# Conformer convolution module: one written order of TensorE, VectorE and ScalarE between its two projections, the last gated block multiplied token tile by token tile, and the low part of the bias row made on GpSimd

## The chip, the cores and the metric

The kernel runs on one core of one Trainium2 chip. The metric is the device time of one execution in microseconds; a median of several executions is given. Engines are named as in the profile: PE (TensorE, matrix multiplications and transposes), ACT (ScalarE), DVE (VectorE), POOL (GpSimd) and SP (SyncE, which here only issues DMAs).

## The reference, cut to what matters

The program is a two-layer trunk over 256 latent tokens (and 256 context tokens in layer one) of width 1024. Layer one mixes tokens with a state-space scan, layer two with a Conformer convolution module; a SwiGLU feed-forward network (FFN) follows each. The change lies in layer two's convolution module:

```
def conformer_conv_module(h, rows, w_pw1, b_pw1, dw_w, dw_b, ln_g, ln_b, w_pw2, b_pw2):
    u = h @ w_pw1 + b_pw1
    u = u[..., :CONF_DIM] * jax.nn.sigmoid(u[..., CONF_DIM:])
    v = axial_dwconv(u, rows, dw_w, dw_b)
    v = jax.nn.silu(layernorm(v, ln_g, ln_b))
    return v @ w_pw2 + b_pw2
...
h_lat = h_lat + g1 * y_lat
```

The 256 tokens are a grid of 4 rows of 64. The depthwise convolution has 31 taps. The first 512 channels are convolved along the rows of the grid ("horizontal": 31 taps within a row of 64). The other 512 are convolved along its columns ("vertical"): a column has 4 tokens, so at most 7 taps matter. The LayerNorm runs over the 1024 channels of one token, so that it needs all eight channel blocks of 128 of a token before it can begin.

## The kernel before, in words

**Numbers.** Every 32-bit projection is done with three TensorE products: a weight tile is split into a high part `wh` (a cast on ACT, L269) and a low part `wl` (a subtraction on DVE, L282), the activation likewise into `xmh` and `xml` (L298, L299), and L293 to L295 add wh·xmh, wl·xmh and wh·xml. A weight tile of 128x1024 thus costs a DMA issued by SP (L267), one ACT instruction and one DVE instruction. The raw tiles have a ring of buffers, so that a late tile's DMA waits until an earlier tile's subtraction has read its buffer.

**First projection.** `tok_proj` (L725) multiplies one of four blocks j of 256 value and 256 gate channels: four weight tiles q, and for each the 6 matmuls of token tile 0 and the 6 of token tile 1, 48 matmuls of 512 columns in all. The tokens stand on the partitions of the result `acc`. ACT copies each token tile of it to `ug` (L1119). After the second weight tile of the next block, PE turns the block before (transposes to `ps`, L250), ACT makes the sigmoid of the gate half (`sig`, L1106) and DVE multiplies (L1108). Blocks j = 0 and 1 give the channel blocks 0 to 3 (into `upad`, padded for the row convolution), j = 2 and 3 the blocks 4 to 7 (into `uver`).

**Depthwise convolution.** A vertical block is one ACT instruction (L1086) and six DVE instructions (L1089) that each add one tap to `cv`. Of the horizontal blocks, block 0 is done wholly on DVE (31 taps, L1139, in two alternating sums `cv` and `odd` that L1141 adds). Blocks 1 and 2 are done wholly on PE and block 3 to 20 of its 31 taps: `upad` goes out to DRAM and comes back as four shifted copies `u4` (DMAs, L1148 and L1150), and `horizontal` (L1153) multiplies these with small diagonal matrices (L1159), 32 matmuls for each block and token tile (20 for block 3). Two rows of the grid are one token tile, 128 columns. ACT moves the result of blocks 1 and 2 to `cv` (L1163), DVE adds that of block 3 (L1165). In the trace a matmul of 32-bit data counts as two, so that 32 of them read "x64".

**LayerNorm and second projection.** For each token tile, `stats` turns two channel blocks at a time to have tokens on partitions (L250, into `acc`) and takes BN_STATS of each 256 channels (DVE, L194). `root` joins them (L198, `var` on L450, `rstd` on GpSimd, L443). `rows` normalizes (L204), `channels` turns it back (L250) and applies gain, bias and SiLU on ACT (L216), `split` makes xmh and xml. Then `project` (L505) multiplies with eight tiles of w_pw2 into four result quarters (2 token tiles by 2 halves of the channels), after two matmuls for each quarter that put in the bias from the two rows `bh` and `bl` (L543). The last four weight tiles come quarter by quarter, "ends". Each quarter is multiplied with the gate row `grow` (L562) and added to the stream `h` (L566); the first FFN norm follows. `grow` comes by a GpSimd DMA (L429) that is written to be issued after the newest `rstd`.

**What sets the order.** Around the first projection only PE's order is written out; the other engines are placed by a scheduler by priority. From the LayerNorm on, a written order of tokens holds for PE, DVE, ACT and POOL together: `LNO`, where `s02` is stats of token tile 0 for the channel blocks 4 and 5, `r` is root, `m` rows, `c` channels, `x` split, `h30` the horizontal block 3 for token tile 0, `W0` the load of w_pw2's tile 0 with its cast, `w0` its subtraction, and `t` a load of ACT's table for SiLU. Then `ORDER` takes over: `R00` is L562/L566 of token tile 0 and channel half 0, `T` the transposes of the FFN norm. `CO` puts one horizontal, block 1 of token tile 0, ahead of `LNO`. The weights w_pw2 4 to 7 are placed by the scheduler, whose freedom is limited by `LF`.

Of the kernel before, what the change touches and what calls it, by code (L numbers as in the profile page):

```python
# [47 lines left out]
LF = (4, 8, "x01"),  # L48
# [4 lines left out]
CO = (1, 0, 2),  # L53
LNO = "W0 w0 W1 w1 s02 s12 h20 h30 t00 s03 s00 s01 r00 W2 W3 s13 h11 m00 c00 m01 w2 c01 h21 x00 w3 s10 x01 m02 c02 m03 c03 x02 x03 h31 s11 r10 m10 c10 m11 c11 x10 m12 x11 m13 c12 x12 c13 x13"
# [121 lines left out]
class LayerNorm:  # L176
# [31 lines left out]
    def channels(self, p, g, b):  # L208
# [14 lines left out]
class Trunk:  # L223
# [501 lines left out]
    def tok_proj(self, src, xh, xl, by_tile=False, between=lambda: None):  # L725
# [345 lines left out]
    def conformer(self, es, xh, xl, h, then):  # L1071
# [12 lines left out]
        def vertical(blk, u):  # L1084
            o = rows(cv[:, blk])
            self.vmark = nc.scalar.activation(out=o, in_=u, func=AF.Identity, scale=w(15, blk), bias=col(PC_DWB + blk)).ins  # L1086
            for d in (-3, -2, -1, 1, 2, 3):
                a, b = max(0, -d), 4 - max(0, d)
                j = nc.vector.scalar_tensor_tensor(out=o[:, a:b], in0=u[:, a + d:b + d], scalar=w(15 + d, blk),  # L1089
                                                   in1=o[:, a:b], op0=ALU.mult, op1=ALU.add)  # L1090
            return j.ins
# [4 lines left out]
        def gated(j, ug):  # L1096

            for b in range(2):
                blk = 2 * j + b
                pt = self.bank()  # L1100
                for s in range(2):
                    for tt in range(2):
                        self.transpose(pt[:, s * 256 + tt * P:s * 256 + tt * P + P],
                                       ug[:, tt, s * 256 + b * P:s * 256 + b * P + P])
                sig = cp.tile([P, 256], F32, name="sig", bufs=2)
                nc.scalar.activation(out=sig, in_=pt[:, 256:512], func=AF.Sigmoid, bias=col(PC_BPW1 + 8 + blk))  # L1106
                u = rows(up[:, blk, 0:376]) if blk < 4 else cp.tile([P, 4, 64], F32, name="uver", bufs=4)
                nc.vector.scalar_tensor_tensor(out=u[:, :, 15:79] if blk < 4 else u, in0=rows(pt[:, 0:256]),  # L1108
                                               scalar=col(PC_BPW1 + blk), in1=rows(sig), op0=ALU.add, op1=ALU.mult)
# [199 lines left out]
```

## Time and profile before

| | us |
|---|---|
| median of 3 runs | 891.5 |
| lowest, highest | 891.26, 891.66 |
| the profiled execution | 889.17 |
| its span in the profile | 887.4 |
| first matmul of block j = 3 | 623.7 |
| last matmul of block j = 3 | 637.7 |
| first matmul of the second projection | 659.1 |
| first transposes of the FFN norm (T00) | 686.96 |

The span of the profiled execution is 1.77 us shorter than its time; the times in the views are counted from the span's start. The program takes the region from 623 to 687 us once. The mean granted clock of TensorE over the whole span is 0.989 of the full speed. PE is busy for 853.3 us of the span (96%), DVE for 665.2, ACT for 506.6 and POOL for 50.6. Rows of a timeline read: start, duration, engine, line, operation, result and sources, and in brackets how long the engine had been idle ahead of it and what ended that.

### The profile page before, as it was taken

What the parts mean: (1) busy time and instruction counts of PE and PEld (TensorE: products, weight loads), DVE (VectorE), ACT (ScalarE), POOL (GpSimd) and SP (SyncE); (2) the same over time, 40 slices, a digit from 0 to 9 for tenths busy, and PEclk for the clock granted to TensorE, in tenths of its full rate; (3) what the DMA queues carried; (4) which work ended last, traced back from release to release, by engine and by line L of the source; (5) the groups of instructions that cost most, each with busy time, mean ns of one, the idle gap of its engine ahead of it and who ended that gap; (6) DMA issues with size and microseconds to landing.
All of it is one profiled execution on the core that took longest, in us unless ns stands there. A gap on an engine that the chain in (4) does not pass through costs nothing.

```text
span 887.4 us, 12716 instructions
## 1 busy us (share of the span) xinstructions
PE 853.3 (96%) x4634; PEld 650.0 (73%) x4634; DVE 665.2 (75%) x1095; ACT 506.6 (57%) x851; POOL 50.6 (6%) x78
## 2 busy tenths in 40 slices
PE   8999999999999999899999999999989999999996
PEld 4576776767677777677888877878767788888885
DVE  3378689897788989879888899677966895555434
ACT  4276988786777987465434444557353754444321
POOL 1001010101011011110000000010001000000000
PEclk9999999999999999989999999999989999999999
DMA  9757856758454445548999888828635497555521
GB/s 342 312 168 253 258 186 197 249 159 262 137 184 167 162 159 179 164 147 308 384 331 368 313 324 325 277 76 296 162 132 202 144 332 255 174 187 188 188 76 47
DMA packets 55873, 194.59 MB, mean 219 GB/s; under 512 B 6666, under 2 KB 9170, under 8 KB 54787
## 3 DMA queue, kind: packets, MB, share of 16 engines
q1 hardware_dynamic: 54338, 190.00, 62.5%
q0 software_dynamic: 896, 2.28, 0.8%
q10 hardware_dynamic: 576, 1.51, 0.6%
q8 instruction: 36, 0.59, 0.3%
q14 instruction: 27, 0.21, 0.1%
HBM read 191.94 MB, written 1.82 MB: 218 GB/s over the span
## 4 chain that ended last, share of the span: by engine, by line
PE 61%; DVE 17%; ACT 6%; DMA 5%; issue 3%; POOL 2%; POOLq 0%; SPq 0%; DVEq 0%; ACTq 0%
PE acc L295 17%; PE acc L294 17%; PE acc L293 17%; DVE wl L282 4%; DVE bx L722 3%; PE ps L250 2%; ACT wh L269 2%; PE ps L970 1%; PE ps L1000 1%; DMA wraw<-in_w_z_dram 1%; DMA wraw<-in_w_pw_dram 1%; PE ps L1159 1%; POOL yw L1014 1%; DMA emat<-edram 1%; PE ps L1008 1%
## 5 line engine op out<-in xcount | busy, mean ns | idle before, releaser
L282 DVE TENSOR_TENSOR wl<-wraw,wh 128x1024 fp32r<-128x1024 f32 (+2 forms) x229 | 269.5, 1183 | 96.8 <-ACT wh L269 96.1
L269 ACT CAST wh<-wraw 128x1024 fp32r<-128x1024 f32 (+2 forms) x229 | 231.1, 1017 | 164.3 <-PE acc L295 70.2
L293 PE MATMUL acc<-wh,xmh 128*128 128x512 f32 x544 | 218.6, 402 | 1.7 <-ACT bx L715 1.4
L295 PE MATMUL acc<-wh,xml 128*128 128x512 f32 x544 | 214.5, 395 | 0.9 <-DVE xml L299 0.8
L294 PE MATMUL acc<-wl,xmh 128*128 128x512 f32 x544 | 214.4, 394 | 0.5 <-DVE wl L282 0.4
L293 PEld LDWEIGHTS acc<-wh,xmh 128*128 128x128 f32 x544 | 102.2, 188 | 29.8 <-issue 4.8
L295 PEld LDWEIGHTS acc<-wh,xml 128*128 128x128 f32 x544 | 102.2, 188 | 26.4 <-DVE xml L299 3.4
L294 PEld LDWEIGHTS acc<-wl,xmh 128*128 128x128 f32 x544 | 102.4, 188 | 22.4 <-DVE wl L282 1.8
L293 PE MATMUL acc<-xmh,wh 128*128 128x512 f32 (+1 forms) x192 | 77.4, 403 | 0.0
L295 PE MATMUL acc<-xmh,wl 128*128 128x512 f32 (+1 forms) x192 | 75.8, 395 | 0.3 <-DVE wl L282 0.3
L294 PE MATMUL acc<-xml,wh 128*128 128x512 f32 (+1 forms) x192 | 75.9, 395 | 0.0
L722 DVE SCALAR_TENSOR_TENSOR bx<-bxraw,pc,bx 128x508 f32<-128x508 f32 (+1 forms) x96 | 68.0, 743 | 5.4 <-ACT bx L715 3.4
L294 PE MATMUL acc<-wl,midh 128*128 128x512 f32 x176 | 69.6, 395 | 0.8 <-DVE wl L282 0.8
L382 DVE SCALAR_TENSOR_TENSOR araw<-araw,srow 128x1024 f32<-128x1024 f32 x56 | 68.1, 1218 | 1.6 <-DMA araw<-in_ada_wt_dram 1.6
L295 PE MATMUL acc<-wh,midl 128*128 128x512 f32 x176 | 69.2, 393 | 0.0
L293 PE MATMUL acc<-wh,midh 128*128 128x512 f32 x176 | 65.9, 394 | 0.0
L293 PEld LDWEIGHTS acc<-xmh,wh 128*128 128x128 f32 (+1 forms) x192 | 35.7, 186 | 13.4 <-issue 5.1
L295 PEld LDWEIGHTS acc<-xmh,wl 128*128 128x128 f32 (+1 forms) x192 | 35.6, 186 | 9.3 <-issue 1.2
L294 PEld LDWEIGHTS acc<-xml,wh 128*128 128x128 f32 (+1 forms) x192 | 35.8, 186 | 8.6 <-issue 1.4
L294 PEld LDWEIGHTS acc<-wl,midh 128*128 128x128 f32 x176 | 33.1, 188 | 10.2 <-DVE wl L282 2.9
L293 PEld LDWEIGHTS acc<-wh,midh 128*128 128x128 f32 x176 | 33.0, 188 | 7.4
L295 PEld LDWEIGHTS acc<-wh,midl 128*128 128x128 f32 x176 | 33.0, 188 | 7.3
(218 smaller groups left out, 1096.2 us busy)
## 6 DMA issues: line engine op xcount, KB each, us to landing
wraw<-in_ffn_in_dram SPq DMA_DIRECT2D x88, 512.0 KB, 5.2
araw<-in_ada_wt_dram SPq DMA_DIRECT2D x56, 512.0 KB, 5.6
wraw<-in_ffn_out_dram SPq DMA_DIRECT2D x44, 512.0 KB, 3.5
wraw<-in_w_xb_dram SPq DMA_DIRECT2D x32, 384.0 KB, 3.9
wraw<-in_ada_w_dram SPq DMA_DIRECT2D x24, 512.0 KB, 4.4
emat<-edram SPq DMA_DIRECT2D x8, 1536.0 KB, 8.0
wraw<-in_w_pw_dram SPq DMA_DIRECT2D x24, 512.0 KB, 4.8
araw<-in_ada_dram SPq DMA_DIRECT2D x16, 512.0 KB, 8.4
```

What stands on the lines that cost most here:

```text
L250: self.nc.tensor.transpose(out, in_, self.ident[0:n, 0:n])
L269: nc.scalar.copy(out=wh[:, :n], in_=raw[:, :n])
L282: self.nc.vector.tensor_tensor(out=wl, in0=raw, in1=wh.bitcast(F32), op=ALU.subtract)
L293: mm(out=out, lhsT=ah, rhs=bh, start=first, stop=False)
L294: mm(out=out, lhsT=ah, rhs=bl, start=False, stop=False)
L295: mm(out=out, lhsT=al, rhs=bh, start=False, stop=last)
L382: self.nc.vector.scalar_tensor_tensor(out=raw, in0=raw, scalar=1.0, in1=self.srow, op0=ALU.mult, op1=ALU.mult, accum_out=col[:, k])
L722: nc.vector.scalar_tensor_tensor(out=o[:, :, a:b], in0=r[:, :, a + d:b + d], scalar=w(k), in1=o[:, :, a:b], op0=ALU.mult, op1=ALU.add)
L970: nc.tensor.matmul(out=ph, lhsT=bt[:, tt], rhs=xw[:, tt], start=tt == 0, stop=tt == 1)
L1000: nc.tensor.matmul(out=po[64 * j:64 * j + 64, d * 256:d * 256 + 256], lhsT=h0[:, d, c], rhs=cc, start=True, stop=True, tile_position=(0, 6 ...
L1008: nc.tensor.matmul(out=py[64 * j:64 * j + 64, p2, q * P:q * P + P], lhsT=xs[:, tt, hl * 64:hl * 64 + 64], rhs=e[:, hl, slot], start=slot i ...
L1014: nc.gpsimd.tensor_tensor(out=w, in0=eo[:, :, 0:256], in1=eo[:, :, 256:512], op=ALU.add)
```

## The change

It has four parts. **(a)** The last block j = 3 is multiplied by token tiles: all 24 matmuls of token tile 0 first, then those of token tile 1. Tile 0 is copied and turned between the matmuls of tile 1 (`begin`); the copy and transposes of tile 1, the gating and the verticals are a token `G` of the order below. The transposes of a block go ahead of both its gatings, and the verticals behind both. **(b)** The horizontal taps on DVE and the shifted copies (`shift`) are written after the gating of block j = 1 and not after the last block. **(c)** `CO` is gone, and the written order for PE, DVE, ACT and POOL starts at the end of block 3. It holds all horizontals; block 1 of token tile 0 and block 3 of token tile 1 are each done in two calls of one grid row (64 columns; `h101`, `h111`, `h321`, `h331`). The table load no longer waits for a mark, the loads W1 to W3 and the subtractions stand at other places, and `LF` makes the casts and subtractions of the w_pw2 tiles 4 to 7 wait for both `x01` and `c01`. **(d)** The subtraction that makes `bl` goes to GpSimd.

```
-LF = (4, 8, "x01"),
+LF = 4, 8, "x01"
...
-CO = (1, 0, 2),
-LNO = "W0 w0 W1 w1 s02 s12 h20 h30 t00 s03 s00 s01 r00 W2 W3 s13 h11 m00 c00 m01 w2 c01 h21 x00 w3 s10 x01 m02 c02 m03 c03 x02 x03 h31 s11 r10 m10 c10 m11 c11 x10 m12 x11 m13 c12 x12 c13 x13"
+LNO = ("h101 G h111 h202 W0 h302 t00 W1 s02 s00 s01 W2 h122 s03 r00 w0 W3 h222 m00 m01 h321 c00 c01 m02 m03 x00 w1 x01 "
+       "c02 c03 h331 w2 x02 x03 w3 s12 s10 s13 s11 r10 m10 m11 c10 x10 c11 x11 m12 m13 c12 x12 c13 x13")
...
         if by_tile:
             for q in range(4):
                 mm(q, ws[q], 1)
+                if q == 1:
+                    first(pa[0])
...
+            for u in us:
+                if u[0] >= 4:
+                    vertical(*u)
...
+        def horizontal(blk, r0, nr):
+            if (blk, r0) == (1, 1):
+                pcv = held.pop()
+            else:
+                pcv = self.pa.tile([P, 512], F32, name="pa") if blk == 1 and r0 == 0 else self.bank()
+            n, u4 = HC[blk], shifted[blk]
+            x = pcv[:, r0 % 2 * 64:(r0 % 2 + nr) * 64]
...
+        def begin(p):
+            ug = cp.tile([P, 2, 512], F32, name="ug", bufs=2)
+            nc.scalar.copy(out=ug[:, 0], in_=p)
+            pts = [self.bank() for _ in range(2)]
+            turned(3, ug, (0,), pts)
+            last.append((ug, pts))
...
-                pa = self.tok_proj(t["w_pw1"][j], xh, xl, j == 0, lambda: last and gated(*last.pop()))
+                pa = self.tok_proj(t["w_pw1"][j], xh, xl, j in (0, 3), before, begin if j == 3 else lambda p: None)
...
-                    nc.vector.tensor_tensor(out=brow[1], in0=raw[0:1], in1=brow[0].bitcast(F32), op=ALU.subtract)
+                    nc.gpsimd.tensor_tensor(out=brow[1], in0=raw[0:1], in1=brow[0].bitcast(F32), op=ALU.subtract)
...
+                elif tok[0] == "G":
+                    ug, pts = last.pop()
+                    nc.scalar.copy(out=ug[:, 1], in_=pa[1])
+                    turned(3, ug, (1,), pts)
+                    gated(3, pts)
+                    continue
...
                 elif tok[0] == "t":
-                    with tc.issue_after(self.vmark):
-                        nc.scalar.activation(out=cp.tile([P, 2], F32, name="table"), in_=self.mhalf, func=AF.Silu)
-        self.count, self.fences = 4, [(a, b, ends if m is None else (marks[m],)) for a, b, m in LF]
+                    nc.scalar.activation(out=cp.tile([P, 2], F32, name="table"), in_=self.mhalf, func=AF.Silu)
+        self.count, self.fences = 4, [(LF[0], LF[1], (marks[LF[2]], marks["c" + LF[2][1:]]))]
```

**What moves on ACT** behind the last gating. Before, from the base instruction of the verticals on (L1086; `wh_6391` and `wh_6397` are the weight tiles 4 and 5 of w_pw2, `ps_6000` is horizontal block 1 of token tile 0):

```order
L1086 ACTIVATE cv_5513<-uver_5906,pc_92 128x256
L1086 ACTIVATE cv_5513<-uver_5922,pc_92 128x256
L1163 ACTIVATE cv_5513<-ps_6060,pc_92 128x128
L1201 ACT_TABLE_LOAD
L1201 ACTIVATE table_6116<-mhalf_94 128x2
L269 CAST wh_6135<-wraw_6134 128x1024
L269 CAST wh_6140<-wraw_6139 128x1024
L269 CAST wh_6391<-wraw_6390 128x1024
L269 CAST wh_6397<-wraw_6396 128x1024
L1163 ACTIVATE cv_5513<-ps_6000,pc_92 128x128
```

And after the change (`pa_5977` is horizontal block 1 of token tile 0, `ps_6070` block 2; `wh_6105`, `wh_6134`, `wh_6151` and `wh_6200` are the tiles 0 to 3):

```order
L1090 ACTIVATE cv_5513<-uver_6017,pc_92 128x256
L1090 ACTIVATE cv_5513<-uver_6021,pc_92 128x256
L1171 ACTIVATE cv_5513<-pa_5977,pc_92 128x128
L1171 ACTIVATE cv_5513<-ps_6070,pc_92 128x128
L271 CAST wh_6105<-wraw_6104 128x1024
L1245 ACT_TABLE_LOAD
L1245 ACTIVATE table_6131<-mhalf_94 128x2
L271 CAST wh_6134<-wraw_6133 128x1024
L271 CAST wh_6151<-wraw_6150 128x1024
L1171 ACTIVATE cv_5513<-ps_6155,pc_92 128x128
```

Both horizontals of token tile 0 that ACT moves now stand ahead of the table load, and the four casts that stood ahead of the second one stand behind both, with the tiles 4 to 7 further down.

**What moves on SP.** The DMA queue before, from the third pair of shifted copies on (`wraw_6390` to `wraw_6408` are the tiles 4 to 7 of w_pw2):

```order
L1148 DMA udram_5993<-upad_5514 128x380
L267 DMA wraw_6390<-in_w_pw2_dram 128x1024
L267 DMA wraw_6396<-in_w_pw2_dram 128x1024
L1150 DMA u4_5994<-udram_5993 32x4x376 x4
L368 DMA araw_6746<-in_ada_wt_dram 128x1024
L267 DMA wraw_6402<-in_w_pw2_dram 128x1024
L267 DMA wraw_6408<-in_w_pw2_dram 128x1024
```

And after the change (`wraw_6444` to `wraw_6462` are these four tiles, `araw` are tiles of the modulation weights of a later stage, whose buffers are those of the diagonal matrices of the horizontals):

```order
L1145 DMA udram_5812<-upad_5514 128x380
L1147 DMA u4_5813<-udram_5812 32x4x376 x4
L370 DMA araw_6800<-in_ada_wt_dram 128x1024
L269 DMA wraw_6444<-in_w_pw2_dram 128x1024
L370 DMA araw_6820<-in_ada_wt_dram 128x1024
L370 DMA araw_6847<-in_ada_wt_dram 128x1024
L269 DMA wraw_6450<-in_w_pw2_dram 128x1024
L269 DMA wraw_6456<-in_w_pw2_dram 128x1024
L269 DMA wraw_6462<-in_w_pw2_dram 128x1024
```

All four tiles 4 to 7 now stand behind the first `araw` tile, three of them behind three such tiles, and the two that stood ahead of the last shifted copies no longer do.

**What moves on DVE** at the second token tile's statistics. After the change the rows from the fourth weight's subtraction to `var` are (`wl_6201` is tile 3, `wl_6452`, `wl_6458` and `wl_6464` are the tiles 5, 6 and 7):

```order
L284 TENSOR_TENSOR wl_6201<-wraw_6199,wh_6200 128x1024
L194 BN_STATS bnst_6321<-acc_6322 128x6
L194 BN_STATS bnst_6321<-acc_6326 128x6
L284 TENSOR_TENSOR wl_6452<-wraw_6450,wh_6451 128x1024
L194 BN_STATS bnst_6321<-acc_6322 128x6
L194 BN_STATS bnst_6321<-acc_6326 128x6
L284 TENSOR_TENSOR wl_6458<-wraw_6456,wh_6457 128x1024
L198 BN_AGGR bnmv_6336<-bnst_6321 128x2
L284 TENSOR_TENSOR wl_6464<-wraw_6462,wh_6463 128x1024
L452 TENSOR_SCALAR var_6338<-bnmv_6336 128x1
```

Before, all these subtractions stood ahead of the last BN_STATS, and the first residual (L562) behind every `nrm` (L204) of the LayerNorm and behind three subtractions of the FFN's weights. Now the subtractions of the tiles 6 and 7 stand between the last BN_STATS and `var`, and the residual (L564, of `acc_6384` and `grow`) ahead of the last `nrm` of the LayerNorm.

More of the change, by code (lines that the diff above doesn't have):

```diff
@@ L723, in conv_silu, with tok_proj @@
                                            in1=o[:, :, a:b], op0=ALU.mult, op1=ALU.add)
-    def tok_proj(self, src, xh, xl, by_tile=False, between=lambda: None):
+    def tok_proj(self, src, xh, xl, by_tile=False, between=lambda: None, first=lambda p: None):
         pa = [self.abank() for _ in range(2)]
@@ L1098, in gated @@
+        def gated(j, pts):
+            us = []
             for b in range(2):
                 blk = 2 * j + b
[L1100 to L1104, printed above, removed]
                 sig = cp.tile([P, 256], F32, name="sig", bufs=2)
-                nc.scalar.activation(out=sig, in_=pt[:, 256:512], func=AF.Sigmoid, bias=col(PC_BPW1 + 8 + blk))
+                nc.scalar.activation(out=sig, in_=pts[b][:, 256:512], func=AF.Sigmoid, bias=col(PC_BPW1 + 8 + blk))
@@ new lines, in conformer, with before @@
+        last, held = [], []
+        def before():
+            if last:
+                j, ug = last.pop()
+                pts = [self.bank() for _ in range(2)]
+                turned(j, ug, (0, 1), pts)
+                gated(j, pts)
+                if j == 1:
+                    shift()
+        def begin(p):
+            ug = cp.tile([P, 2, 512], F32, name="ug", bufs=2)
+            nc.scalar.copy(out=ug[:, 0], in_=p)
+            pts = [self.bank() for _ in range(2)]
+            turned(3, ug, (0,), pts)
+            last.append((ug, pts))
@@ L1153, in horizontal @@
-        def horizontal(blk, r0, nr):
-            n, pcv, u4 = HC[blk], self.bank(), shifted[blk]
-            out, x = cv[:, blk, r0 * 64:(r0 + nr) * 64], pcv[:, 0:nr * 64]
-            for i in range(n):
-                for g in range(4):
-                    nc.tensor.matmul(out=x[32 * g:32 * g + 32], lhsT=self.dk[blk - 1][:, g * 8 + i],
-                                     rhs=rows(u4[:, g])[:, r0:r0 + nr, 4 * i:4 * i + 64], start=i == 0, stop=i == n - 1,
-                                     tile_position=(0, 32 * g))
-            if 4 * n >= CONF_K:
-                nc.scalar.activation(out=out, in_=x, func=AF.Identity, bias=col(PC_DWB + blk))
-            else:
-                nc.vector.tensor_tensor(out=out, in0=x, in1=out, op=ALU.add)
@@ L1167, in conformer @@
-        for blk, r0, nr in CO:
-            horizontal(blk, r0, nr)
+                    nc.gpsimd.tensor_tensor(out=brow[1], in0=raw[0:1], in1=brow[0].bitcast(F32), op=ALU.subtract)
         one = lambda c: self.pc[:, c:c + KD].unsqueeze(2)
```

93 lines of the change are left out of this document (57 added, 36 removed).

## The prediction

> **What bounds the kernel now.** I read the page's chain of waits by engine, then PE's timeline between 623 and 690 us, the only stretch that the change touches apart from part (d), and then ACT's, which ends the longest gap.
>
> ```profile
> PE 61%; DVE 17%; ACT 6%; DMA 5%; issue 3%; POOL 2%; POOLq 0%; SPq 0%; DVEq 0%; ACTq 0%
> ```
>
> PE sets most of the end. In the stretch itself its timeline has four idle gaps (in brackets):
>
> ```profile
> 637.68 0.30 PE L250 MATMUL acc<-konst,cv 128*128 128x128 f32 x1 [2.15 <-DVE cv L1089]
> 650.21 0.47 PE L250 MATMUL acc<-konst,cv 128*128 128x128 f32 x1 [3.60 <-ACT cv L1163]
> 651.21 1.11 PE L250 MATMUL acc<-konst,cv 128*128 128x128 f32 x4 [0.53 <-DVE bnst L194]
> 652.25 3.44 PE L1159 MATMUL ps<-u,araw 128*32 128x128 f32 x64
> 656.21 1.96 PE L1159 MATMUL ps<-u,araw 128*32 128x128 f32 x64
> 659.10 0.50 PE L293 MATMUL acc<-wh,xmh 128*128 128x512 f32 x1
> 669.93 0.41 PE L250 MATMUL ps<-konst,nrm 128*128 128x128 f32 x2 [0.45 <-DVE nrm L204]
> 684.63 0.40 PE L295 MATMUL acc<-wh,xml 128*128 128x512 f32 x1
> 686.72 0.40 PE L295 MATMUL acc<-wh,xml 128*128 128x512 f32 x1
> 686.96 0.82 PE L250 MATMUL ps<-konst,nrm 128*128 128x128 f32 x6
> ```
>
> The first gap is a transpose for the statistics, placed ahead of block 3's last matmul, that waits for DVE's verticals. The second waits for ACT, whose timeline shows why:
>
> ```profile
> 644.62 1.28 ACT L1201 ACT_TABLE_LOAD   x1
> 646.03 3.87 ACT L269 CAST wh<-wraw 128x1024 fp32r<-128x1024 f32 x4
> 649.80 0.36 ACT L1163 ACTIVATE cv<-ps,pc 128x128 f32<-128x128 f32 x1
> ```
>
> The copy of horizontal block 1 at 649.80 stood behind a table load and four weight casts. The T00 transposes at 686.96 follow the last matmul at its usual pitch (nine from 684.63 to 686.72, 0.232 each), so PE is what leads up to them, and T00 is my anchor.
>
> Idle time is not all: the granted clock (second last columns: PEclk, DMA share, GB/s) falls after gaps.
>
> ```profile
> 329.00:331.00 2.00, 0.87 (x5) 0.41 (x4) 2.00 (x4) 1.98 (x3) 0.00 (x0) 1.00 0.00 0
> 638.00:646.00 8.00, 8.00 (x180) 6.87 (x178) 6.80 (x21) 4.38 (x8) 0.00 (x0) 0.79 0.02 5
> 652.20:655.60 3.40, 3.40 (x65) 2.95 (x64) 3.01 (x7) 0.00 (x0) 0.55 (x1) 0.54 0.02 5
> 639.00:640.00 1.00, 1.00 (x6) 0.50 0.00 0
> ```
>
> Of the 8 us from 638.0, 0.21 x 8 / 0.5 = 3.4 us ran at half clock. After the 3.60 us gap the horizontal at 652.25 takes 3.44 us, the same at full clock 1.96. Half the busy time at half clock is lost: 3.4/2 = 1.7, and of 0.47 + 1.11 + 3.4 us after 650.2 about 2.3. So PE loses 2.15 + 3.60 + 0.53 + 0.45 = 6.7 us idle and 4.0 us to the clock between block 3 and T00, 10.7 in all.
>
> **The change part by part.** *What PE does.* Counted in both orders from block 3's first matmul to T00, PE has the same 141 matmuls of 512 columns, 8 for the bias, 48 transposes, and 168 horizontals; only, 52 of the latter (32 of block 1, 20 of block 3) are done as 104 of 64 columns. Each of 128 columns costs 1.96/32 = 61 ns. No 64-column one is in the trace. Bounds: half of that each (extra 0) and the same (52 x 61 = 3.2 us). The nearest rows are another small-matmul line at two widths:
>
> ```profile
> 12.39 0.65 PE L342 MATMUL pa<-araw,sc 128*32 128x128 f32 x16
> 78.16 0.64 PE L342 MATMUL pa<-wraw,sc 128*32 128x256 f32 x8
> ```
>
> Less a last one's 0.27 and 0.39 us, these pace records at 25 and 36 ns, 0.09 ns a column. 64 columns less take 6 ns off a horizontal record's 31 ns, and 25 ns was the least seen, so 27 ns: 208 x 27 - 104 x 31 ns = 2.4 us, my value. [...]
>
> So T00 moves by 10.7 - 2.4 - (idle and half clock after) = 8.3 less what is lost anew. I walk through the new order for that.
>
> *Block 3's end.* Same matmuls, plus the first half of `h101` (32 x 54 ns) in place of other small ones: 637.7 as before. Then comes a bare wait: G copies tile 1 before turning it, with nothing written between.
>
> ```profile
> 638.24 0.58 ACT L1119 COPY ug<-acc 128x512 f32<-128x512 f32 x1 [2.99 <-PE acc L295]
> 640.57 0.47 ACT L1106 ACTIVATE sig<-ps,pc 128x256 f32<-128x256 f32 x1 [1.74 <-PE ps L250]
> 641.08 0.48 DVE L1108 SCALAR_TENSOR_TENSOR uver<-ps,pc,sig 128x256 f32<-128x256 f32 x1 [0.45 <-ACT sig L1106]
> 642.24 3.55 DVE L1089 SCALAR_TENSOR_TENSOR cv<-uver,pc,cv 128x64 f32<-128x64 f32 x12
> 614.98 1.00 DVE L1139 SCALAR_TENSOR_TENSOR cv<-upad,pc,cv 128x256 f32<-128x256 f32 x2
> 625.97 0.49 DVE L1139 SCALAR_TENSOR_TENSOR odd<-upad,pc,odd 128x256 f32<-128x256 f32 x1
> 626.37 0.49 DVE L1139 SCALAR_TENSOR_TENSOR cv<-upad,pc,cv 128x256 f32<-128x256 f32 x1
> ```
>
> With the copy's 0.58 and the handovers it is **0.9** us idle. Only four transposes remain, so the sigmoid starts near 639.05, 1.5 earlier. DVE's taps and block 2's verticals, which (b) moves, stand ahead of this gating in both orders; two BN_STATS (0.4 each) no longer do, and DVE was free 0.45 before its row above, so it is there at about 639.6.
>
> *Verticals.* Last are 12 again, but each now depends on the one before it: a dependent pair takes 0.52 us a piece (1.00 for two) where alternating ones start 0.40 apart, so 12 cost 1.2 more: 640.7 to 645.4. Then `h302`'s add and the handover; the transposes s01 run at about 646.4. PE by then has done h111 1.75, h202 1.97, h302 1.23, two pairs of transposes: free at 644.5. New wait: **1.9** us, in place of the first gap; ACT's table load and casts are behind both horizontal copies now, so the 3.60 goes. What is late next is the norm: `h122` (1.97), s03, root, then by DVE's order `w0`'s subtraction, and nrm at 651.0; before:
>
> ```profile
> 653.52 0.99 DVE L204 TENSOR_SCALAR nrm<-acc,bnmv,rstd 128x256 f32<-128x256 f32 x2 [0.33 <-POOL rstd L443]
> ```
>
> PE covers that with `h222` and `h321`, waits **0.9** around the normalized blocks, and reaches the second projection at 656.9, 2.2 before 659.10.
>
> *Weights 4 to 7 and the gate row.* These were prefetched or cast early; now tile 4's DMA waits for a buffer until `w0`'s subtraction (651.05), and tile 7 for tile 4's. Durations:
>
> ```profile
> 656.16 3.06 SPq L267 DMA_DIRECT2D wraw<-in_w_pw_dram  x2
> 660.84 1.05 ACT L269 CAST wh<-wraw 128x1024 fp32r<-128x1024 f32 x1 [2.24 <-DMA wraw<-in_w_pw_dram]
> 668.65 0.55 POOL L443 TENSOR_TENSOR rstd<-var,mhalf 128x1 f32<-128x1 f32 x1 [15.17 <-DVE var L450]
> 669.15 0.64 POOL L429 DMA_DIRECT2D grow<-gdram x1
> DMA to landing us min/median/max: 5.2/5.9/7.6
> 680.50 0.68 DVE L562 TENSOR_TENSOR res<-acc,grow 128x512 f32<-128x512 f32 x1
> ```
>
> Landing takes 660.84 - 656.16 = 4.7. Tile 4: 655.75, cast and subtraction to 658.45; tile 7's DMA then, 663.15, cast 1.05, subtraction 1.2 (a quarter of the row of four further down): 665.4. `var` of token tile 1 stands behind that subtraction: rstd ends at 666.6, the gate row's DMA follows and lands at 672.5 (5.9, the last row but one). R00 needs it and ends at 673.2. It now frees the bank for the last quarter's bias, where PE stands from 671.35: **1.85** us, new. Queued behind R00 on DVE is the last nrm; its transposes stand behind that bias on PE anyway. After it: bias 0.65, transposes 0.25, 44 matmuls x 0.232 = 10.2, so T00 at 684.3 by PE, and 684.7 (**0.4** idle) by its own residual, square and norm.
>
> *Part (d).* Off DVE goes this; its neighbour on GpSimd is a subtract-like row of half the columns:
>
> ```profile
> 598.62 1.21 DVE L1125 TENSOR_TENSOR bl<-wraw,bh 1x1024 fp32r<-1x1024 f32 x1
> 603.70 4.98 DVE L282 TENSOR_TENSOR wl<-wraw,wh 128x1024 fp32r<-128x1024 f32 x4 [2.75 <-ACT wh L269]
> L1029 POOL TENSOR_TENSOR sqacc<-sqacc,eo 128x512 f32<-128x512 f32 x8 | 11.9, 1488 | 25.6 <-ACT eo L1028 25.6
> ```
>
> DVE waits 2.75 us for a cast right after, so its 1.2 us buys nothing (gain bounds 0 to 1.2). GpSimd takes 1.5 to 3.0, from 595; the second projection needs it 60 us later. Cost 0.
>
> *Sum.* Lost anew: 0.9 + 1.9 + 0.9 + 1.85 + 0.4 = 5.95. 10.7 - 2.4 - 5.95 = 2.3 us gain, as 686.96 - 684.7. The profiled execution has 889.17 us (span 887.4, 1.77 around it); 2.3 off gives 886.9. The median lies 2.3 above that execution, so the forecast is 891.5 - 2.3 = **889.2**. About 0.2% (1.8 us) separates a change from none.
>
> **The rivals.**
>
> *A, the clock.* Do 1.9 us gaps cost half-clock spells? Another gap of such length does:
>
> ```profile
> 374.49 0.50 PE L293 MATMUL acc<-wh,yh 128*128 128x512 f32 x1 [1.99 <-ACT yh L1033]
> 376.00:377.00 1.00, 1.00 (x3) 0.81 (x4) 0.26 (x1) 0.66 (x1) 0.00 (x0) 0.50 0.91 365
> 330.83 0.50 PE L294 MATMUL acc<-wl,yh 128*128 128x512 f32 x1 [1.13 <-DVE wl L282]
> ```
>
> Behind 1.99 us the clock was 0.50, behind 1.13 still 1.00. Spells last 3.4 us or a multiple and seem to start on a grid of 3.4 us, so a gap that a grid line halves may pass; continued from 638.4 the grid has lines at 645.2 and 672.5, inside both of my gaps. But 1 us of error moves them off. One spell costs up to 1.7: gain 0.6, 890.9; both: 892.6. [...]
>
> *B, slower.* One chain leads from `w0` through two serial weight transfers and the gate row to R00: 4.7 + 4.7 + 5.9 = 15.3 us of landing, and it binds by 1.85 already, so each further us costs one. From 17.6 us on the kernel is slower; at 6 + 6 + 7.6 = 19.6 (the gate row's maximum) it is 4.3 later: 893.5. For it: three `araw` transfers are issued among them. Against: each of my landings is one that was measured.
>
> *C, faster.* With landings of 3.5, 3.5 and 5.2, chain and gap vanish: 889.2 - 1.85 - 0.35 = 887.0.
>
> **How the numbers follow.** Forecast 0.45, own range 887.5 to 890.6 (64-column extra 0 to 3.2, handovers); A 0.24, both spells a third of it; B 0.15; C 0.16. Faster by over 0.2% (below 889.7): three quarters of the forecast, C, a little of A: 0.51. Slower: B and the worst of A: 0.17. No change 0.32. The range reaches past C and to B's price: 886.0 to 893.3, with B's tail and C's beyond it.
>
> **What would show it.** ACT's horizontal copies right after PE, no 3.6 us gap; the sigmoid near 639, nrm near 651; s01 behind a 1 to 2 us gap; the gate row landing near 672.5 and PE idle then; T00 near 684.7; horizontal records of 64 columns at 25 to 28 ns. I would be wrong if the projection began after 658, if clock spells stayed at 0.5 for 6 us as before, or if tiles 5 to 7 held up PE's "ends" ahead of the gate row.

## The result: 893.55 us against 889.56, slower by 0.65% where 0.26% faster was forecast

The changed kernel takes 893.55 us (median of 20 executions, 890.66 to 899.21), the kernel before 889.56 us (median of 20, 883.05 to 891.66). The ratio of the executions is 1.0065, with a 95% interval of [1.0045, 1.0084]: slower by 4.0 to 7.5 us. The forecast was 889.2 us with a range of 886.0 to 893.3, so both the sign and the range were missed. The forecast had started from 891.5, the median of three executions; among the twenty these three are near the top, and 2.3 us off 889.56 would have been 887.3. One execution of one variant below (the kernel before with GpSimd's subtraction alone) took 2134.87 us and is left out of that variant's ratio.

Where did the time come from? PE's timeline of the kernel before gives the marks that the comparison uses: the first four transposes of the norm ahead of the convolution module, the eight transposes that turn block j = 0, and the eight that turn block 1.

```profile
590.92 0.67 PE L250 MATMUL ps<-konst,nrm 128*128 128x128 f32 x4 [0.81 <-ACT wh L269]
605.33 1.03 PE L250 MATMUL ps<-konst,ug 128*128 128x128 f32 x8
617.27 1.04 PE L250 MATMUL ps<-konst,ug 128*128 128x128 f32 x8
```

I call the stretch from the first mark to the second S1 (14.41 us before) and the one from the third to T00 S2 (686.96 - 617.27 = 69.69 us before). Between the two lie 11.9 us in each of the fourteen profiles of this study, and from T00 to the end of the span 200.4 to 200.5 us. So in the profiles the changed stretches are S1 and S2 alone. What lies ahead of S1 has the same work in all kernels, but takes 588.6 to 597.4 us; the same kernel before was profiled twice and took 590.9 and 595.7. Single times thus scatter by more than what is looked for, and S1 and S2 are read beside the medians.

This is PE's timeline after the change, from the same marks to T00, with the waits of 0.3 us and more:

```profile
593.28 0.66 PE L252 MATMUL ps<-konst,nrm 128*128 128x128 f32 x4 [0.82 <-ACT wh L271]
600.12 0.50 PE L295 MATMUL acc<-wh,xmh 128*128 128x512 f32 x1 [1.56 <-DVE xmh L300]
601.59 0.80 PE L297 MATMUL acc<-wh,xml 128*128 128x512 f32 x1 [0.73 <-DVE xml L301]
602.18 0.63 PE L295 MATMUL acc<-wh,xmh 128*128 128x512 f32 x1
610.92 1.04 PE L252 MATMUL ps<-konst,ug 128*128 128x128 f32 x8
622.85 1.03 PE L252 MATMUL ps<-konst,ug 128*128 128x128 f32 x8
640.10 1.10 PE L1161 MATMUL pa<-u,araw 128*32 128x64 f32 x64
643.66 0.66 PE L252 MATMUL ps<-konst,ug 128*128 128x128 f32 x4 [0.68 <-ACT ug L1225]
651.36 0.41 PE L252 MATMUL acc<-konst,cv 128*128 128x128 f32 x2 [2.17 <-DVE bnst L194]
651.70 3.10 PE L1161 MATMUL ps<-u,araw 128*32 128x128 f32 x64
658.66 0.86 PE L252 MATMUL ps<-konst,nrm 128*128 128x128 f32 x4 [0.64 <-DVE nrm L204]
670.69 0.50 PE L296 MATMUL acc<-wl,xmh 128*128 128x512 f32 x1 [0.45 <-DVE wl L284]
672.49 0.50 PE L296 MATMUL acc<-wl,xmh 128*128 128x512 f32 x1 [0.83 <-DVE wl L284]
673.74 0.50 PE L296 MATMUL acc<-wl,xmh 128*128 128x512 f32 x1 [0.30 <-DVE var L452]
680.64 0.49 PE L545 MATMUL acc<-bh,onerow 1*128 1x512 f32 x1 [1.05 <-DVE res L564]
692.45 0.87 PE L252 MATMUL ps<-konst,nrm 128*128 128x128 f32 x6 [0.72 <-DVE nrm L106]
```

S1 is now 610.92 - 593.28 = 17.64 us, 3.2 more; S2 is 692.45 - 622.85 = 69.60, 0.1 less. The forecast had S1 unchanged and S2 2.3 shorter. The waits of 1.56 and 0.73 us lie in S1, and behind them a matmul of 512 columns takes 0.63 instead of 0.39: the granted clock there was 0.50. The reader should see two things more. The 3.60 us wait of before, behind ACT's table load and casts, is gone, as forecast. In its place and that of the 2.15 us stand eight others in S2, the largest of 2.17 us, as against four before.

GpSimd and VectorE at the two places that matter, each from its engine's timeline. GpSimd:

```profile
596.98 2.94 POOL L1207 TENSOR_TENSOR bl<-wraw,bh 1x1024 fp32r<-1x1024 f32 x1 [3.99 <-ACT bh L1206]
656.46 1.48 POOL L445 TENSOR_TENSOR rstd<-var,mhalf 128x1 f32<-128x1 f32 x1 [56.54 <-DVE var L452]
673.82 0.55 POOL L445 TENSOR_TENSOR rstd<-var,mhalf 128x1 f32<-128x1 f32 x1 [15.88 <-DVE var L452]
674.32 0.66 POOL L431 DMA_DIRECT2D grow<-gdram  x1
```

VectorE:

```profile
596.48 1.22 DVE L284 TENSOR_TENSOR wl<-wraw,wh 128x1024 fp32r<-128x1024 f32 x1
597.62 2.44 DVE L300 CAST xmh<-modv 128x256 fp32r<-128x256 f32 x1
645.86 4.49 DVE L1093 SCALAR_TENSOR_TENSOR cv<-uver,pc,cv 128x64 f32<-128x64 f32 x12 [0.28 <-ACT cv L1090]
656.30 1.22 DVE L284 TENSOR_TENSOR wl<-wraw,wh 128x1024 fp32r<-128x1024 f32 x1
657.98 0.99 DVE L204 TENSOR_SCALAR nrm<-acc,bnmv,rstd 128x256 f32<-128x256 f32 x2 [0.45 <-POOL rstd L445]
679.90 0.69 DVE L564 TENSOR_TENSOR res<-acc,grow 128x512 f32<-128x512 f32 x1 [1.62 <-DMA grow<-gdram]
```

The cast of `xmh` takes 0.28 to 0.30 us in the kernel before (0.43 at most, in six places of its first 50 us). Here one takes 2.44 and ends at 600.06, just behind the end of GpSimd's subtraction (599.92). GpSimd's 2.94 us hold a wait as well: the weight's subtraction on VectorE runs from 596.48 to 597.70, and from there to the end of GpSimd's instruction it is 2.22 us. And where `w0`'s subtraction runs on VectorE from 656.30 to 657.52, the power that makes `rstd` on GpSimd takes 1.48 instead of 0.55. The two engines hold each other up; the experiments below test it.

### The profile page after: what moved, and what is told of

The parts are those of the page before. It is cut to its first block, busy times and chain, and to the rows that moved or that the text cites. A ratio compares the mean times of both kernels' runs of the same rounds, so it can differ in the third digit from the quotient of the medians.

```text
span 892.9 us, 12915 instructions
## 1 busy us (share of the span) xinstructions
PE 856.0 (96%) x4736; PEld 650.2 (73%) x4738; DVE 666.5 (75%) x1095; ACT 507.1 (57%) x851; POOL 54.0 (6%) x79
## 4 chain that ended last, share of the span: by engine, by line
PE 69%; DVE 14%; ACT 6%; DMA 6%; issue 3%; POOL 2%; SPq 0%; POOLq 0%; DVEq 0%; ACTq 0%
PE acc L297 19%; PE acc L295 19%; PE acc L296 19%; DVE bx L724 3%; DVE wl L284 3%; PE ps L252 2%; PE pa L344 2%; DMA emat<-edram 2%; PE ps L1004 1%; DMA wraw<-in_ffn_out_dram 1%; PE ps L974 1%; ACT wh L271 1%; PE ps L1012 1%; POOL yw L1018 1%; DVE yl L1038 1%
```

## The experiments

Every kernel below was compared with runs of the kernel before made beside it; its ratio is the quotient with the 95% interval. S1 and S2 are from its one profile, in us. S1 + S2 is 84.1 in both profiles of the kernel before. The changed kernel was measured twice, and its two intervals overlap, so what a variant gains on it is read against both.

| kernel | ratio to before | S1 | S2 |
|---|---|---|---|
| changed | 1.0065 [1.0045, 1.0084] | 17.64 | 69.60 |
| changed, again | 1.0048 [1.0026, 1.0070] | 16.64 | 68.62 |
| changed, bias row's low part on VectorE | 1.0021 [1.0004, 1.0039] | 14.38 | 69.54 |
| changed, gate row early | 1.0022 [1.0002, 1.0042] | 17.62 | 67.34 |
| changed, w0 and w1 early | 1.0056 [1.0031, 1.0081] | 17.69 | 68.61 |
| changed, verticals alternating | 1.0043 [1.0020, 1.0067] | 16.57 | 68.51 |
| changed, GpSimd's subtraction in four | 1.0030 [1.0006, 1.0054] | 16.56 | 70.23 |
| changed, VectorE and gate row | 0.9993 [0.9974, 1.0012] | 14.43 | 68.80 |
| all four | 0.9976 [0.9960, 0.9992] | 14.37 | 64.28 |
| all four but GpSimd's subtraction | 0.9981 [0.9960, 1.0002] | 16.60 | 65.70 |
| before, again | 1.0017 [0.9990, 1.0044] | 14.43 | 69.65 |
| before, GpSimd's subtraction alone | 0.9992 [0.9968, 1.0015] | 16.60 | 65.20 |
| before, no low part | 0.9972 [0.9952, 0.9991] | 15.20 | 65.35 |

### Part (d) undone, and part (d) alone

```
-                    nc.gpsimd.tensor_tensor(out=brow[1], in0=raw[0:1], in1=brow[0].bitcast(F32), op=ALU.subtract)
+                    nc.vector.tensor_tensor(out=brow[1], in0=raw[0:1], in1=brow[0].bitcast(F32), op=ALU.subtract)
```

> The changed kernel with the bias row's low part back on VectorE, all else kept. Theory P (GpSimd's 2.94 us subtraction holds something that VectorE's cast of xmh needs, so that the cast took 2.44 us in place of 0.29, PE stood 1.56 and 0.73 us and then ran at half clock): from the transposes of the first norm (L252, four of them) to the transposes of block j = 0 the stretch is 14.4 us as before, not 17.6, and the kernel is about 3.2 us faster than the changed one, 890 us, equal to the kernel before within 1 us. Rival Q (the raw buffer that GpSimd holds longer delays a weight's DMA, or the stretch merely differs from run to run): the stretch stays over 16.5 us or the cast stays long.

Measured: 890.36 us, ratio 1.0021 against the changed kernel's 1.0065, and S1 14.38 as before. All casts take 0.29 us. Theory P holds: this one instruction makes S1 3.3 us longer in the first profile of the changed kernel, where a half-clock spell follows the waits, and 2.3 in the second, where none does. By ratio it is worth 0.44% against the first set of the changed kernel and 0.27% against the second.

The reverse, the kernel before with only this line moved to GpSimd:

> The kernel before with only part (d): the bias row's low part on GpSimd. Theory P: the same cast (or the first VectorE instruction of its kind beside GpSimd's subtraction) takes about 2.4 us, the stretch grows from 14.4 to 17 to 18 us and the kernel is about 3 us slower than before (1.003). Rival Q: no change within 1 us.

Measured: 888.14 us, ratio 0.9992 [0.9968, 1.0015]. The lock (VectorE's cast is held until GpSimd's instruction ends) is there, VectorE's timeline of this kernel first, then PE's:

```profile
593.00 2.45 DVE L298 CAST xmh<-modv 128x256 fp32r<-128x256 f32 x1
```

```profile
595.50 0.50 PE L293 MATMUL acc<-wh,xmh 128*128 128x512 f32 x1 [1.56 <-DVE xmh L298]
596.97 0.50 PE L295 MATMUL acc<-wh,xml 128*128 128x512 f32 x1 [0.74 <-DVE xml L299]
646.32 0.33 PE L250 MATMUL acc<-konst,cv 128*128 128x128 f32 x1 [3.33 <-ACT cv L1163]
```

S1 grows by 2.2 (without the half-clock spell behind it), but the kernel is not slower, because S2 falls from 69.7 to 65.2. PE's order is the same row by row; what is gone is the 2.15 us wait at block 3's end, the clock spell behind it and half of the spell at the next wait (3.4 us at half clock in place of 6.8). Theory P is right about the lock and was wrong about the sum, 3 us slower. Something in the kernel before pays it back, and that needed a run of its own (below).

### Is it an exclusive lock?

```
+                    for q in range(4):
+                        s = slice(q * 256, q * 256 + 256)
+                        nc.gpsimd.tensor_tensor(out=brow[1][:, s], in0=raw[0:1, s], in1=brow[0].bitcast(F32)[:, s],
+                                                op=ALU.subtract)
```

> The changed kernel with GpSimd's subtraction in four pieces of 256 columns. If VectorE's cast is locked out for the whole of the GpSimd instruction that runs (exclusive, not shared), the cast now takes at most one piece longer, about 0.3 to 1.0 us in place of 2.44, VectorE and GpSimd then alternate, and the stretch S1 is 15 to 16 us. If both merely slow each other down, the cast and its neighbours stretch evenly and S1 stays near 17.6.

GpSimd's four pieces and then VectorE beside them:

```profile
595.37 4.60 POOL L1209 TENSOR_TENSOR bl<-wraw,bh 1x256 fp32r<-1x256 f32 x4 [4.00 <-ACT bh L1206]
```

```profile
596.02 0.82 DVE L300 CAST xmh<-modv 128x256 fp32r<-128x256 f32 x1
596.76 1.75 DVE L284 TENSOR_TENSOR wl<-wraw,wh 128x1024 fp32r<-128x1024 f32 x1
598.44 0.94 DVE L301 TENSOR_TENSOR xml<-modv,xmh 128x256 fp32r<-128x256 f32 x1
599.30 0.82 DVE L300 CAST xmh<-modv 128x256 fp32r<-128x256 f32 x1
```

The four VectorE instructions (0.29, 1.22, 0.42 and 0.29 us when alone) each take 0.52 or 0.53 longer, whatever their own length, and 0.52 is nearly one piece (a quarter of 2.22 is 0.55): each waits for the piece that runs and then takes its usual time. Were the engines slowing each other down, the 1.22 us one would have lost more than the others. GpSimd's pieces take 1.31, 0.77, 1.69 and 0.91 us, the longer the VectorE instruction that stands ahead of them, and together 4.60 instead of 2.94. That is turn by turn, not slower side by side. The other runs show the cast held for as long as the unsplit instruction runs: it takes 2.44 to 2.50 us where GpSimd makes the row in one piece (in all seven of these profiles PE waits 1.56 to 1.63 us for `xmh`), and 0.29 in the six in which it does not. S1 is 16.56, not the 15 to 16 that I expected, the same 16.6 that unsplit ones without a clock spell show: PE's waits are now 1.80 and 0.55 us, both for `xml`. The split is no cure.

### What off VectorE is worth in the kernel before

```
-                    nc.vector.tensor_tensor(out=brow[1], in0=raw[0:1], in1=brow[0].bitcast(F32), op=ALU.subtract)
+        with tc.issue_after(self.pmark):
+            nc.gpsimd.memset(brow[1].bitcast(F32), 0.0)
```

> The kernel before without the bias row's low part (it is left out: zeros are written in its place), so that neither VectorE nor GpSimd makes it. With part (d) alone, the stretch from block 1's transposes to T00 fell from 69.7 to 65.2 us while the one before it grew by 2.2. Theory U (PE came 2.2 us later and so VectorE's verticals of block 2 were in time; VectorE itself gained nothing, since it waits at the next casts anyway): here the gap of about 2 us at block 3's end stays, and the stretch is 69 to 70 us. Theory V (the 1.2 us off VectorE carry over to the verticals): the gap shrinks below 1 us, one clock spell goes, the stretch is 65 to 67 us and the kernel 2 to 4 us faster than before.

Measured: 886.75 us, ratio 0.9972 [0.9952, 0.9991], S2 65.35. At block 3's end PE no longer waits (the transposes for the statistics now stand one matmul earlier in its order):

```profile
636.80 0.39 PE L293 MATMUL acc<-wh,xmh 128*128 128x512 f32 x1
637.03 0.27 PE L250 MATMUL acc<-konst,cv 128*128 128x128 f32 x1
637.06 0.48 PE L294 MATMUL acc<-wl,xmh 128*128 128x512 f32 x1
```

Theory V holds, theory U falls: one VectorE instruction of 1.21 us at 598.62 costs the kernel before some 2.5 us, forty microseconds later, as the wait for the verticals and a spell at half clock behind it. The cover that I had named, VectorE's 2.75 us wait at 603.70, was no cover. (The `memset` that this variant adds on GpSimd costs it something: it stands beside VectorE's `nrm` from 591.68 to 592.77, two of which take 1.69 instead of 0.91, and S1 is 15.20.) A view of SP's waits between 588 and 612 us in the kernel before seems to say why:

```profile
SPq L267 <- DVE bl L1125: 1.1, 1, 1.1
```

SP waited 1.1 us for that very subtraction, as it reads a raw buffer of the weights' ring. But the weight that VectorE waits for at 603.70 is another. Its DMA and its cast are, from SP's and ACT's timelines:

```profile
596.76 0.33 SPq L267 DMA_DIRECT2D wraw<-in_w_pw_dram  x1
```

```profile
602.62 1.05 ACT L269 CAST wh<-wraw 128x1024 fp32r<-128x1024 f32 x1 [2.04 <-DMA wraw<-in_w_pw_dram]
```

It was issued before the subtraction began and landed at 602.60. The DMA that SP issued behind the subtraction, at 599.89, landed at 605.11. So the instruction did not cause that wait, and how its time gets past it is not shown. What the traces do show is where VectorE stands later: the first of the two adds that end its horizontal taps (L1141, L1142 in this variant) starts 26.2 us behind the transposes of block j = 0 in the kernel before, 23.5 without the row and 23.9 with the row on GpSimd (where PE itself comes 2.2 us later).

So part (d) has two effects of like size: off VectorE is worth 2.5 us in the kernel before (3.5 by S1 + S2), and on GpSimd, at this place, it costs 2.2 to 3.3. In the changed kernel the first is worth nothing that shows (S2 is 69.54 with the row on VectorE, 69.60 and 68.62 with it on GpSimd), probably because part (b) leaves VectorE idle for 4.10 us ahead of the last gating, and only the cost stays.

### Was the loss read from the first profile a property of the kernel?

> The kernel before, unchanged, profiled a second time. The forecast took PE's loss between block 3 and T00 from one profile: 6.7 us idle and 4.0 us at half clock. Theory T (that loss depends on where the 3.4 us grid of the clock lies and on whether block 2's verticals come just in time): the stretch from the transposes of block 1 to T00, 69.7 us in the first profile, comes out at 65 to 68 us, with one half-clock spell. Rival: it is 69 to 70 us again, with two spells, and the loss was a property of the kernel.

Measured: S2 69.65, waits of 1.97 and 3.61 us and spells of 3.4 and 6.8 us at half clock, the second of which begins within its wait. Theory T falls. The ledger of 10.7 us lost in the kernel before was read rightly.

### The gate row

```
 elif tok[0] == "r":
+    first = self.pmark
     marks[tok] = n.root()
+    if tok == "r10":
+        self.pmark = first
```

> The changed kernel with the gate row's GpSimd DMA issued behind the first token tile's rstd and not behind the second's. Theory R: the row lands 17 us earlier, R00 no longer waits for it, PE's gap of 1.05 us ahead of the last bias goes, but PE's remaining waits stay; the kernel is about 1 us faster than the changed one. Rival: R00's wait only goes over to another source, and the time stays within 0.5 us.

Measured: 890.56 us, ratio 1.0022, and S2 67.34, 2.3 shorter than in the changed kernel's first profile and 1.3 than in its second. R00 no longer waits, and T00 follows the last matmul without a gap:

```profile
689.52 0.89 PE L252 MATMUL ps<-konst,nrm 128*128 128x128 f32 x6
```

From the first bias to T00 it is 28.3 us against 30.5. In the second profile of the changed kernel it is 29.7. The wait for the gate row thus costs 2.2 in the first, twice the idle time that PE's row shows for it (1.05): the 0.72 ahead of T00 goes with it, and the rest would be that the first matmul behind a stop takes longer (0.50 instead of 0.39).

### w0 and w1 early

```
-h302 t00 W1 s02 s00 s01 W2 h122 s03 r00 w0 W3 h222 ... x00 w1 x01
+h302 t00 W1 s02 s00 s01 w0 W2 w1 h122 s03 r00 W3 h222 ... x00 x01
```

> The changed kernel with the subtractions w0 and w1 moved ahead of the statistics s03 in the written order, where VectorE stood idle for 3.2 us. Theory R (the new loss between 650 and 692 us is that w0 stands between var and nrm: it lengthens rstd on GpSimd from 0.55 to 1.48 us, and it and w1 hold back the buffers of the weight tiles 4 and 5): rstd takes 0.55 us, nrm comes 0.9 us earlier, tiles 4 and 5 are loaded 4 to 7 us earlier, the three gaps of PE for weights (0.45, 0.83, 0.30 us) go, and the kernel is 2 to 3 us faster than the changed one, about 891. Rival S (the loss is the verticals' dependent order and the clock spell behind the 2.17 us gap): less than 1 us faster.

Measured: 893.39 us, ratio 1.0056, no gain that can be told from none. Its rows on GpSimd and PE show why:

```profile
657.38 0.56 POOL L445 TENSOR_TENSOR rstd<-var,mhalf 128x1 f32<-128x1 f32 x1 [56.47 <-DVE var L452]
672.84 0.66 POOL L431 DMA_DIRECT2D grow<-gdram  x1
```

```profile
679.88 0.50 PE L545 MATMUL acc<-bh,onerow 1*128 1x512 f32 x1 [1.77 <-DVE res L564]
```

`rstd` takes 0.56, two of the three waits for weights are gone, the third is 0.24, and R00's wait has grown from 1.05 to 1.77. Its mechanism is as theory R said. Its price was taken back: by the gate row, which was still issued behind the second `rstd`, with a spell of 3.4 us at half clock behind R00's longer wait, and in this profile by a longer wait at s01 (2.52 instead of 2.17) as well.

### Alternating verticals

```
-            for u in us:
-                if u[0] >= 4:
-                    vertical(*u)
+            if j >= 2:
+                for blk, u in us:
+                    nc.scalar.activation(out=rows(cv[:, blk]), in_=u, func=AF.Identity, ...)
+                for d in (-3, -2, -1, 1, 2, 3):
+                    for blk, u in us:
+                        nc.vector.scalar_tensor_tensor(...)
```

> The changed kernel with the last block's verticals in alternating order of the two blocks, as the scheduler had them before. If the dependent order costs what the two rows say (12 in 4.49 us against 3.48), s01 comes 1.0 us earlier and PE's gap of 2.17 us falls to about 1.2; if gap lengths over 1.2 us inside one grid window are what drops the clock, the half-clock spell behind it goes too in some executions. Then 1 to 2.5 us faster than the changed kernel (891 to 892.5), unless the gate row's wait takes it back as it did with w0 and w1 moved (then less than 0.5).

Measured: 892.72 us, ratio 1.0043; PE's two waits in question:

```profile
653.43 0.41 PE L252 MATMUL acc<-konst,cv 128*128 128x128 f32 x2 [1.33 <-DVE bnst L194]
681.79 0.49 PE L545 MATMUL acc<-bh,onerow 1*128 1x512 f32 x1 [1.38 <-DVE res L564]
```

The wait at s01 falls from 2.17 to 1.33 and no half-clock spell follows it; up to the first bias the stretch is 36.8 us instead of 39.1. But the gate row's wait is now 1.38, and behind it comes a spell at half clock. Again the gain stops at the gate row. As the ratios' intervals overlap, the price of this step alone is not settled.

### Together

> The changed kernel with the bias row's low part back on VectorE and the gate row's DMA behind the first rstd. If the two losses are independent, 3.2 and 2.2 us, it is 5.4 us faster than the changed one: 888 us, within 0.3% of the kernel before on either side. If they overlap, 889.5 or more.

Measured: 888.53 us, ratio 0.9993 [0.9974, 1.0012]. The two losses add up as far as the intervals tell (0.44% and 0.43% alone, 0.72% together, against the first set): without them the change is worth nothing measurable, with S2 68.80, of which this profile spends some 10 us at half clock.

> The changed kernel with all four: bias row on VectorE, gate row early, w0 and w1 ahead of s03, verticals alternating. With the gate row out of the way, w0 and w1 should be worth their 0.9 us and the verticals 1.0: 886 us, 0.3% faster than the kernel before. If the wait for weight tiles 6 and 7 takes the place of the gate row, 887.5 or more.

Measured: 886.26 us, ratio 0.9976 [0.9960, 0.9992]: faster than the kernel before by 0.1 to 0.4%, and the fastest complete kernel of this study. S2 is 64.28, with 3.7 us idle and no half-clock spell. The largest waits that are left:

```profile
646.77 0.41 PE L252 MATMUL acc<-konst,cv 128*128 128x128 f32 x2 [1.03 <-DVE bnst L194]
665.56 0.50 PE L296 MATMUL acc<-wl,xmh 128*128 128x512 f32 x1 [0.76 <-DVE wl L284]
```

With GpSimd's subtraction put back into it:

> The fastest version so far (gate row early, w0 and w1 ahead of s03, verticals alternating), but with the bias row's low part on GpSimd as in the change. Theory P: 2 to 3 us slower than with it on VectorE (886.3), 889; S1 16.6 to 17.6 against 14.4. If a later PE start is paid back as in the kernel before with part (d) alone, within 1 us of it.

Measured: 887.72 us, ratio 0.9981 [0.9960, 1.0002], S1 16.60. The cast is held for 2.47 us here too. The medians differ by 1.5 us as theory P says in sign, but the intervals overlap; by ratio alone this run does not tell it from nothing, S1 does.

### The changed kernel again

> The changed kernel, unchanged, profiled a second time, to see which of its losses come in every execution. Expected again: the cast of 2.4 us, rstd of 1.5 us, gaps near 2.2 us at s01, three for the weights, and 1 to 2 us for the gate row; the clock spells may lie elsewhere. S1 16.6 to 17.7 us, block 1's transposes to T00 67 to 70 us.

Measured: 893.79 us, ratio 1.0048 [1.0026, 1.0070]. The cast takes 2.50, `rstd` 1.48, s01's wait is 2.25 and the gate row's 0.99; S1 is 16.64, as no spell follows its waits, and S2 68.62. Of the three waits for weights two came.

## Why the prediction was wrong, point by point

**Part (d), "Cost 0".** This is the step that failed most. GpSimd's duration was sized rightly (1.5 to 3.0, it took 2.94) and the second projection's need of the row, sixty microseconds later, as well. I asked who waits for the result, and not what the instruction holds while it runs. It held VectorE's cast for 2.2 us in the one stretch where PE waits for `xmh` (1.56 and 0.73 us); where a clock spell followed, 1.0 more. Undoing it gives back the difference between 1.0065 (1.0048 in the second set) and 1.0021. The trace of the kernel before could have told me, at the very row (L1029) from which I took GpSimd's duration. One of its eight instructions and VectorE's beside it:

```profile
171.34 1.48 POOL L1029 TENSOR_TENSOR sqacc<-sqacc,eo 128x512 f32<-128x512 f32 x1 [3.31 <-ACT eo L1028]
```

```profile
171.70 1.41 DVE L1034 SCALAR_TENSOR_TENSOR yl<-yw,pc,yh 128x256 fp32r<-128x256 f32 x1
```

In all eight places VectorE's instruction takes 1.21 to 1.52 us, and the next one of the same line, behind GpSimd's end, 0.47.

The other half of the step was wrong too: "its 1.2 us buys nothing" took VectorE's next wait as cover; in the kernel before, leaving the instruction out is worth 2.5 us, by a path that is not shown.

**"10.7 lost" before.** Right, and found again in the second profile.

**The 3.60 us wait goes.** Right: ACT's horizontal copies follow PE at once, the casts come later.

**Block 3's end, "0.9".** 0.68. **s01, "1.9".** 2.17, from the dependent verticals (4.49 us for twelve; I had 4.7), as the step said; with alternating ones it is 1.33.

**The clock.** The forecast put the half-clock spell behind s01's wait into rival A with 0.24, since a grid line would halve the wait. It came in both profiles of the changed kernel and in every one with a wait of 1.97 us or more between block 3 and T00. This is 1.7 us. The spells of one profile lie on a grid of 3.41 us wherever two of them were dated (last section), but it lies elsewhere in each execution: in the changed kernel's first profile one step runs from 648.9 to 652.3 and holds the whole wait. I had continued the grid of an execution of the kernel before, which says nothing about another one.

**nrm, "w0's subtraction" ahead of it.** The order was read; that it also stretches `rstd` by 0.93 (1.48 instead of 0.55) was not. PE waited 0.64 and 0.17 here, 0.1 less than forecast, but `nrm` came 1.4 us later than forecast, counted from block 1's transposes, and PE was late too.

**Weights 4 to 7.** I had them arrive in time (0). PE waited 0.45, 0.83 and 0.30. SP's and ACT's timelines:

```profile
661.93 3.53 SPq L269 DMA_DIRECT2D wraw<-in_w_pw_dram  x3
```

```profile
668.33 1.05 ACT L271 CAST wh<-wraw 128x1024 fp32r<-128x1024 f32 x1 [4.90 <-DMA wraw<-in_w_pw_dram]
```

Landing took 668.33 - 661.93 = 6.4 us and not 4.7, with two `araw` tiles just ahead in the queue. This is the sign of being wrong that the prediction names last, tiles that hold up PE ahead of the gate row, and not rival B: the three landings of B's chain took 3.5, 5.7 and 5.5 us, 14.7 together, where 15.3 was forecast.

**R00, "1.85".** The chain to the gate row was read rightly and taking the wait away is worth 2.3 in S2 against the first profile. The size came out lower partly by luck: counted from block 1's transposes, R00 ended 1.8 us later than forecast, but PE, held up by the weights and the clock, reached the wait 2.7 us later, and so waited 1.05 and not 1.85. Ahead of T00 it waited 0.72 (I had 0.4).

**The 64-column pieces, "2.4".** Mis-sized: 64 records took 1.10 us with the last one's 0.27 (row at 640.10), 13 ns each, as against 27 for 128 columns by the same working (1.96 us for 64, the prediction's row at 656.21): half, so that the extra is a few tenths at most. I had taken the nearest row of another line as my value.

**The sum.** In the first pair of profiles S1 and S2 together were forecast at -2.3 and came out at +3.1, a difference of 5.4 us. Term by term, found less forecast (for the clock, half of a spell's 3.4 us, an estimate): part (d) +3.2, the clock behind s01 +1.7, the weights +1.6, s01 +0.3, T00 +0.3, block 3's end -0.2, nrm -0.1, R00 -0.8, the 64 columns -2.1 (with an extra of 0.3, an estimate: their four rows take 1.10 + 1.10 + 0.73 + 0.77 = 3.70 us in the changed kernel's first profile, one row of 64 and one of 40 records at 128 columns 1.96 + 1.30 = 3.26 in that of the kernel before, so that 0.4 is the most). That is 3.9. Of the 1.5 us left over, 0.4 would be the first matmul behind a stop (0.50 us where others take 0.39, and eight stops instead of four); for the other 1.1 no row stands, and they stay open.

**What stays open.** The medians differ by 4.0 us and the ratio says 5.8, more than the 3.1 of S1 and S2. Of the twelve variants and repeats, most show the same: the ratios of nine stand 1.1 to 3.3 us above what their profiles' S1 + S2 give against 84.1, those of the others within 0.3. Either the kernel before has fewer half-clock spells in most executions than in its two profiles, or the part ahead of S1 takes longer in the changed programs. The clocks on record do not settle the first: the mean granted clock is 0.990 over 35 executions of the kernel before (0.989 and 0.985 in the profiled ones), and 0.989 over 20 and 0.992 over 8 of the changed one (0.988 and 0.990 in the profiled ones), and where the spells lay is known for the profiled ones alone. As for the second, the 588.6 to 597.4 us are too scattered to tell with fourteen profiles.

## What to carry to other kernels

Before moving an instruction to an engine that seems free, ask not only who waits for its result but what it holds while it runs, and which instructions of the neighbour engine stand beside it in the trace at that moment. An idle gap right behind an instruction is no proof that the instruction costs nothing: a run without it tells, and here it told 2.5 us. When two edits each give nothing, look whether both stop at the same later wait: here the gate row took back much of what two reorderings had gained, and only the four together gave 0.24%.

## What the runs showed of the hardware that was not expected

VectorE and GpSimd held each other up by whole instructions, in both directions: a 0.29 us cast took 2.44 beside a 2.94 us GpSimd subtraction, and a 0.55 us GpSimd power took 1.48 beside a 1.22 us VectorE subtraction in both profiles of the changed kernel, and 0.55 or 0.56 without one in those of the kernel before (668.65), of w0 and w1 early (657.38) and of all four (650.82). A GpSimd instruction on one partition (the subtraction of 1x1024) did this as well as one on 128 (L1029, 128x512, in the kernel before, where VectorE's instruction beside it took 1.21 to 1.52 instead of 0.47 in all eight places).

PE's granted clock fell to half for about 3.4 us behind waits as short as these, the first of the changed kernel with the row on VectorE:

```profile
673.37 0.49 PE L545 MATMUL acc<-bh,onerow 1*128 1x512 f32 x1 [1.16 <-DVE res L564]
```

```profile
676.00:678.00 2.00, 2.00 (x6) 1.58 (x5) 1.78 (x3) 2.00 (x3) 0.00 (x0) 0.50 0.00 0
```

A 1.38 us wait did it as well (alternating verticals, at 681.79), while 1.33 at 653.43 and 1.58 at 604.23 in the same profile, 1.58 at 647.83 in that of all four but GpSimd's subtraction, and 1.80 at 599.43 in that with GpSimd's subtraction in four did not. So the length of a wait alone does not decide.

In the six profiles in which two or more spells at half clock were dated in one trace, these begin whole multiples of 3.41 us apart: 638.28 and 648.52 in the kernel before, three steps; 601.13 and 652.33 in the changed kernel, fifteen; 644.58 and 675.30 with the row on VectorE, nine; 600.52 and 651.72 with the gate row early, fifteen; 602.27, 653.47 and 680.78 with w0 and w1 early, fifteen and eight; 647.63 and 657.87 with VectorE and gate row, three. The grid that they lie on stands elsewhere in each execution; a step below is 3.41 us, from one of its lines to the next.

Counted from PE's records over the whole first profiles of the kernel before and of the changed kernel, six steps at full clock held 1.84 us or more of idle time, and each was followed by one at half clock; the other 498 held 1.28 or less, and none was. In nine other profiles, between S1's start and T00, eleven steps with 1.77 us or more were followed by one at half clock, and five with 1.49 to 1.74 were not. Thus the waits for `xmh` and `xml` put 1.84 us of idle time into one step in the first profile of the changed kernel, and a spell followed, but 1.63 us in the second, and none did. That is the difference between S1 of 17.6 and of 16.6. Three steps of the nine profiles with less, and a spell behind them, are not explained: the 1.16 and the 1.38 above, and 1.10 from 654.5 with VectorE and gate row.
